# Two fused transformer blocks: the expert stage's small experts in four column tiles, its activations in other buffers, rows flipped and weight blocks refetched earlier

## The chip, the cores and the metric

The program runs on one core of a Trainium2 chip. The metric is the device time of one execution in microseconds (us); less is better. The times shown are three executions of the kernel before, and one more execution was taken with the hardware profiler.

## What is computed

Two transformer blocks on 512 rows of width 1024, in float32. The change touches only the mixture of experts of the second block, which is

```python
def moe(x, w_router, b_router, w_up, b_up, w_down, b_down):
    xf = x.reshape(-1, D)
    logits = (xf @ w_router + b_router).astype(jnp.float32)
    top_v, top_i = lax.top_k(logits, TOP_K)          # TOP_K = 4 of 32 experts
    w = jax.nn.softmax(top_v, axis=-1)
    ...
    h = lax.ragged_dot(xs, w_up, sizes) + b_up[sorted_e]     # w_up: 1024 x 2048 for each expert
    g, lin = jnp.split(h, 2, axis=-1)
    g = jnp.minimum(g, SWIGLU_LIMIT)
    lin = jnp.clip(lin, -SWIGLU_LIMIT, SWIGLU_LIMIT)
    act = g * jax.nn.sigmoid(SWIGLU_ALPHA * g) * (lin + 1.0)
    y = lax.ragged_dot(act, w_down, sizes) + b_down[sorted_e] # w_down: 1024 x 1024 for each expert
    y = y * w.reshape(-1)[order][:, None].astype(y.dtype)
    return jax.ops.segment_sum(y, tok, num_segments=n).reshape(B, T, D)
```

The 512 rows make 2048 row-expert pairs. Counted with the reference's fixed inputs, twelve experts have more than 64 rows (149, 143, 130, 127, 126, 121, 101, 101, 87, 87, 82 and 74), nine have at most 32, and the other eleven lie between 33 and 63. Nothing of this is known when the program is built: the counts are worked out on the chip, and the program branches on them.

## The kernel before, in words

**Weight blocks.** An expert's weights are read once, as 12 blocks of 1 MiB (128 x 2048 float32): eight of `w_up` and four of `w_down`. All 32 experts' blocks run through one ring of eight raw buffers, so that block n+8 can be fetched only when the buffer of block n is free; `refill(n)` issues that fetch, on SyncE's (SP's) queue, in the order of the program. The raw buffers are halves of four tiles: `b1` holds blocks 0 and 1 of the ring, `pp` 2 and 3, `b3` 4 and 5, `b0` 6 and 7 (the profile writes all but `pp` as `b`). I call an expert's blocks F0 to F11 for a small expert and E0 to E11 for a large one.

**Places.** `order` sorts the experts by row count and gives each a place 0 to 31. Place 0 is expert 0's, a large one here. Large experts (over 64 rows) take the even places 2, 4, ... by falling count, small ones the odd places by rising count. `places` then runs `nP` pairs (here 11) of a small step `few(1 + 2t, paired)` and a large step `expert(2 + 2t)`, in nested `If`s on `nP`, and after them the remaining small experts one after the other (`rest`, a binary tree of `If`s, here from pair 11 on, and a last one). By the counts above, pairs 0 to 8 have a small expert of at most 32 rows, and pairs 9 and 10 one of 33 and 36.

**The small step** multiplies in float32, the expert's 64 rows standing in TensorE as weights and the block moving through: two column tiles of 64 columns side by side, 256 columns of the block each (`halves`). Right after a block's matmuls its buffer is refilled. Its activations are transposed into `hf`, which lies in tile `y`, the tile from which `finish` scatters results with an adding indirect DMA.

**The large step** works in split precision: ScalarE rounds a block to `wh`, VectorE makes the rest `wl` (`split`, lines 219 and 220), into one of four pairs of buffers (`pairs`, by n % 4), and TensorE takes three products for each of four 128-row pieces (`part`). Blocks are split two ahead of their use; E0 and E1 are split in the small step before (`unfold` at i = 10, 11). A split frees the raw buffer: E2 to E11 are refilled behind their split, but E0 and E1 only in the large step, behind E2's and E3's. `ahead` transposes ("flips") the next step's gathered rows: a large expert's rows at i = 8 and 9 of the small step. In pairs 0 to 3 (`SECOND`) the large step also computes rows 128 to 159 of its expert with `second`, in float32 and four column tiles of 32, from the raw block, and so keeps each raw buffer until then.

**Order of the work.** The program is written with a framework that schedules each engine's instructions and puts in the waits. The lines that touch the change:

```python
            if i < 10:
                self.split(*self.pairs[(n + 2) % self.PAIRS], self.raw(n + 2))
                if not two:
                    self.refill(n + 2)
            if i < 2 and not two:
                self.refill(n)
```

Of the kernel before, what the change touches and what calls it, by code (L numbers as in the profile page):

```python
# [25 lines left out]
NE, TT = 32, 128  # L26
# [131 lines left out]
class K:  # L158
# [944 lines left out]
    RAW, PAIRS = 8, 4  # L1103
# [38 lines left out]
    def moe(self):  # L1142
        tc, nc, a = self.tc, self.nc, self.a
        with ExitStack() as es:
# [52 lines left out]
            for n in range(2):  # L1197
                self.unfold(n)
# [10 lines left out]
    def places(self, srt):  # L1209
# [41 lines left out]
        pairs(0)  # L1251
# [106 lines left out]
    def finish(self, e, big):  # L1358

        nc, m = self.nc, self.m  # L1360
        sl, i = m["sl"][e // 4 % 2], e % 4
        if big:
            for c in range(2):
                nc.scalar.activation(m["y"][0][:, 512 * c:512 * c + 512], self.bank(e, 8 + c), AF.Copy, scale=sl["w"][:, i:i + 1])
            self.scatter(m["y"][0], sl, i)
        else:
            for c in range(2):
                p, w = self.bank(e, 8 + c), sl["w"][:64, i:i + 1]
                nc.scalar.activation(m["y"][0][:64, 512 * c:512 * c + 256], p[:64, :256], AF.Copy, scale=w)
                nc.vector.tensor_scalar(m["y"][0][:64, 512 * c + 256:512 * c + 512], p[64:, :256], w, None, op0=OP.mult)  # L1370
            self.scatter(m["y"][0], sl, i, 64)
# [44 lines left out]
    def expert(self, e, two=False):  # L1416
# [7 lines left out]
        for i in range(12):  # L1424
            n = e * 12 + i
            if i < 10:
                self.split(*self.pairs[(n + 2) % self.PAIRS], self.raw(n + 2))
                if not two:
                    self.refill(n + 2)
            if i < 2 and not two:  # L1430
                self.refill(n)
# [5 lines left out]
            if i == 0 and e:  # L1437
                self.finish(e - 1, False)
# [6 lines left out]
        self.finish(e, True)  # L1445
# [16 lines left out]
    def second(self, i, e):  # L1462
# [6 lines left out]
        act, hf = [m["y"][0][:, 256 * a:256 * a + 256] for a in range(2)]  # L1469
# [35 lines left out]
    def halves(self, p, x, i, e):  # L1505
# [5 lines left out]
        o = p[:64, :256], p[64:, :256]  # L1511

        cut = lambda w, n: self.cut(w, up, j, n, 2)
        if up and kh == 0:
            b = self.bup.bitcast(F32)[:, 512 * (j // 2):512 * (j // 2) + 512]
            for n in range(2):
                nc.tensor.matmul(o[n], self.m["one"][e % 2].bitcast(F32)[:, j % 2, :64], cut(b, n), start=True, stop=False)
        w = self.raw(e * 12 + i).rearrange("p (k f) -> p k f", k=4)
        for k in range(4):
            for n in range(2):  # L1520
                nc.tensor.matmul(o[n], x(4 * kh + k), cut(w[:, k], n), start=not up and kh == k == 0, stop=kh == 1 and k == 3)  # L1521

    def few(self, e, paired=False, second=False):
# [3 lines left out]
        xf, act = m["xf"], m["act"][0][:, :512]  # L1527
        hf = m["y"][0][:, :512].rearrange("p (t a r) -> p t a r", t=4, a=2)
        h = lambda k: hf[:, k % 2, k // 2] if k < 4 else hf[:, k % 2 + 2, k // 2 - 2]
        for i in range(12):  # L1530
            n = e * 12 + i
            self.halves(self.bank(e, i), (lambda k: xf[:, k]) if i < 8 else h, i, e)
            self.refill(n)
            if i > 9 and (paired or e == NE - 1):
                self.unfold(n + 2)
            if i == 0 and e and e % 2 == 0:
                self.finish(e - 1, False)
            self.ahead(e, i, 8, paired)
            if i == 3 and second:
                self.further(e + 1)  # L1540
            if i in (3, 5, 7):
                j = i // 2
                pg, pl = [self.bank(e, k)[:, :256] for k in (0, 2)] if j == 1 else \
                    [self.bank(e, i)[:, 128 * k:128 * k + 128] for k in range(2)]
                self.gated(pg, pl, self.side(act, j, 64))
            if i in (5, 8, 9):
                t0, t1 = {5: (0, 2), 8: (2, 3), 9: (3, 4)}[i]
# [3 lines left out]
                nc.vector.tensor_copy(hf[:, t0:t1].rearrange("p t a r -> p t (a r)"), p[:, :t1 - t0])  # L1551
            if e == NE - 1 and i == 6:
                self.last_rows(e)
        if e % 2 == 0:
            self.finish(e, False)
# [3 lines left out]
    def ahead(self, e, i, at, both):  # L1559
# [5 lines left out]
        for f in [e + 2] * (i == 2) + [1] * (i == 1 and e == 0):  # L1565
            if f < NE:
                self.gather(m["xg"][f % 2], m["sl"][f // 4 % 2], f % 4, 64 if f % 2 or at == 8 and e else 128)
# [167 lines left out]
    def order(self, c):  # L1735
# [13 lines left out]
        gt = S2[:, 160:222].rearrange("p (a e) -> p a e", a=2)  # L1749
        col = [S2[:, 284 + i:285 + i] for i in range(12)]  # L1750
        kc, big, q1, g, sb, far, ex = col[:7]
        r4 = S2[:, 296:298]
        r, na = [r4[:, i:i + 1] for i in range(2)]
# [45 lines left out]
        v.memset(of[:, 3:7], 0.0)  # L1799
# [139 lines left out]
```

## Time and profile before

| what | us |
|---|---|
| three executions: median (lowest to highest) | 2599.25 (2596.93 to 2601.3) |
| the profiled execution's own time | 2600.15 |
| its span, first to last instruction | 2598.1 |
| pairs 0 to 3, from the first small step's first matmul (window in Rows 2) | 335.8 |
| pair 4 | 72.8 |
| pairs 5 to 9 | 348.2 |
| pair 10 and the wait behind it | 84.7 |
| the nine small experts behind the pairs | 285.1 |

The span is divided by the first matmul of a pair's small step (line 1517), which can be read off TensorE's timeline. Everything ahead of 1385.4 us is the first block, the attention of the second, routing and place 0.

### The profile page before, as it was taken

The page shows a single profiled execution, that of the slowest core. Times are in us where ns is not written, and L with a number is a line of the kernel's source. Part 1 is how long each engine was busy: PE and PEld are TensorE (multiplying, and loading weights), DVE is VectorE, ACT ScalarE, POOL GpSimd, SP SyncE. Part 2 cuts the span into 40 slices and gives each one's busy share as a digit, 9 for nine tenths or more (in the row PEclk, how much of TensorE's full clock was granted, in tenths as well). Part 3 has the DMA queues.
Part 4 walks back from the last instruction along what each step waited for, and adds up shares of the span by engine and source line. Part 5 has one row for each costly group of instructions (what it writes and reads, how often), then busy time and mean ns, then how long its engine had stood idle before and what let it go on. Part 6 is the DMA issues. An engine that isn't in the chain of part 4 may idle for free. (4 is left out here: it accounts for less than half of the span.)

```text
span 2598.1 us, 41846 instructions
## 1 busy us (share of the span) xinstructions
PE 2425.4 (93%) x17042; PEld 1941.2 (75%) x17042; DVE 1326.2 (51%) x2473; ACT 1043.5 (40%) x1578; POOL 174.5 (7%) x184
## 2 busy tenths in 40 slices
PE   7999999999999999999989999999999999788888
PEld 5789987898898898898976676666666666554557
DVE  6767753344333344557585466445656666121135
ACT  5755552223223324557353344334444444111133
POOL 0021100000000000000010010110001000000000
PEclk9999999999999999999979999999999999899999
DMA  4122222322222222220378889989999999799990
GB/s 160 65 90 78 74 70 89 127 86 88 98 93 86 98 70 83 75 71 17 109 271 324 305 317 333 341 301 367 381 378 392 385 403 373 294 399 400 407 376 33
DMA packets 86474, 552.63 MB, mean 213 GB/s; under 512 B 11799, under 2 KB 12951, under 8 KB 24936
## 3 DMA queue, kind: packets, MB, share of 16 engines
q1 hardware_dynamic: 71280, 508.33, 50.6%
q0 software_dynamic: 8352, 29.76, 4.7%
q10 hardware_dynamic: 6616, 11.53, 1.3%
q8 instruction: 142, 2.33, 0.4%
q14 instruction: 84, 0.69, 0.1%
HBM read 530.03 MB, written 19.55 MB: 212 GB/s over the span
## 5 line engine op out<-in xcount | busy, mean ns | idle before, releaser
L245 PE MATMUL mm<-b,wh 128*128 128x512 f32 (+1 forms) x1840 | 512.8, 365 | 1.7 <-ACT b L222 0.8
L245 PEld LDWEIGHTS mm<-b,wh 128*128 128x128 f32 x1840 | 328.8, 190 | 65.4 <-issue 3.4
L245 PE MATMUL mm<-b,wl 128*128 128x512 f32 (+2 forms) x920 | 335.2, 365 | 1.3 <-DVE wl L205 1.3
L245 PE MATMUL mm<-wh,b 128*128 128x256 f32 x1488 | 284.3, 287 | 1.5 <-DVE b L675 0.8
L205 DVE TENSOR_TENSOR wl<-raw,wh 128x2048 fp32r<-128x2048 f32 x81 | 185.5, 2290 | 176.2 <-ACT wh L204 176.2
L204 ACT ACTIVATE wh<-raw 128x2048 fp32r<-128x2048 f32 x81 | 155.1, 1915 | 261.2 <-PE mm L245 248.8
L245 PEld LDWEIGHTS mm<-wh,b 128*128 128x128 f32 x1488 | 235.9, 191 | 4.6 <-DVE b L675 1.2
L245 PE MATMUL mm<-wl,b 128*128 128x256 f32 x744 | 213.0, 286 | 1.0 <-DVE wl L205 1.0
L220 DVE TENSOR_TENSOR wl<-b,wh 128x2048 fp32r<-128x2048 f32 x74 | 169.2, 2288 | 65.4 <-ACT wh L219 62.4
L245 PEld LDWEIGHTS mm<-b,wl 128*128 128x128 f32 (+1 forms) x920 | 174.6, 190 | 31.8 <-DVE wl L205 2.2
L1521 PE MATMUL lg<-b,xf 128*64 128x256 f32 x1280 | 154.3, 389 | 14.7 <-DMA b<-w_up 10.1
L219 ACT ACTIVATE wh<-b 128x2048 fp32r<-128x2048 f32 x74 | 141.0, 1908 | 61.8 <-DMA b<-w_up 30.8
L245 PEld LDWEIGHTS mm<-wl,b 128*128 128x128 f32 x744 | 141.9, 191 | 2.5 <-DVE wl L205 1.3
L1521 PEld LDWEIGHTS lg<-b,xf 128*64 128x64 f32 x1280 | 94.3, 139 | 65.7 <-DMA b<-w_up 15.9
L1521 PE MATMUL lg<-b,b 128*64 128x256 f32 x1024 | 130.7, 394 | 7.5 <-DMA b<-w_dn 7.2
L213 POOL TENSOR_TENSOR rs<-rm,c_nhalf 128x1 f32<-128x1 f32 (+3 forms) x52 | 53.0, 1021 | 1158.9 <-DVE rm L211 1150.6
L1521 PEld LDWEIGHTS lg<-b,b 128*64 128x64 f32 x1024 | 76.0, 141 | 49.1 <-issue 11.5
L1345 ACT ACTIVATE sg<-mm,seven 128x128 f32<-128x128 f32 (+2 forms) x48 | 21.8, 455 | 223.2 <-PE mm L1521 180.9
L1521 PE MATMUL mm<-pp,xf 128*64 128x256 f32 x640 | 84.3, 388 | 4.6 <-DMA pp<-w_up 4.5
L1347 DVE SCALAR_TENSOR_TENSOR sg<-lg,sg 128x256 f32<-128x256 f32 (+1 forms) x48 | 19.2, 399 | 127.6 <-ACT sg L1346 127.6
L1521 PE MATMUL mm<-b,xf 128*64 128x256 f32 x640 | 74.8, 383 | 7.0 <-DMA b<-w_up 7.0
L1345 ACT ACTIVATE sg<-lg,seven 128x256 f32<-128x256 f32 (+1 forms) x48 | 21.7, 452 | 146.1 <-PE lg L1521 118.4
(534 smaller groups left out, 4597.9 us busy)
## 6 DMA issues: line engine op xcount, KB each, us to landing
b<-w_up SPq DMA_DIRECT2D x190, 1024.0 KB, 6.7
b<-w_dn SPq DMA_DIRECT2D x96, 1024.0 KB
pp<-w_up SPq DMA_DIRECT2D x64, 1024.0 KB, 13.4
raw<-w_in SPq DMA_DIRECT2D x39, 1024.0 KB, 4.9
pp<-w_dn SPq DMA_DIRECT2D x32, 1024.0 KB, 14.2
raw<-w_up SPq DMA_DIRECT2D x16, 1024.0 KB, 5.8
raw<-w_down SPq DMA_DIRECT2D x16, 1024.0 KB, 4.8
raw<-w_out SPq DMA_DIRECT2D x8, 1024.0 KB, 4.8
```

The lines of the kernel that those rows point to most:

```text
L204: nc.scalar.activation(wh, raw, AF.Copy)
L205: nc.vector.tensor_tensor(wl, raw, wh.bitcast(F32), op=OP.subtract)
L213: self.nc.gpsimd.tensor_tensor(r, m, self.c["nhalf"][:, :n], op=OP.pow)
L219: nc.scalar.activation(hi, src, AF.Copy)
L220: nc.vector.tensor_tensor(lo, src, hi.bitcast(F32), op=OP.subtract)
L245: self.nc.tensor.matmul(ps, l, r, start=(i == 0), stop=(i == n - 1))
L1345: nc.scalar.activation(sg, pg, AF.Relu, scale=-1.0, bias=m["seven"][:rows, 0:1])
L1347: nc.vector.scalar_tensor_tensor(sg, pg, 7.0, sg, op0=OP.min, op1=OP.mult)
L1521: nc.tensor.matmul(o[n], x(4 * kh + k), cut(w[:, k], n), start=not up and kh == k == 0, stop=kh == 1 and k == 3)
```

## The change

- `few` takes a number `of` of column tiles. With `of=4` it keeps 32 rows and sends 128 columns of the block to each of four tiles (`pieces`, in place of `halves`); `finish` then evacuates four pieces of 32 x 128 for each bank and scatters 32 rows.
- `order` also counts the experts of at most 32 rows, and `places` runs nested `If`s on `nT` (the smaller of that count and `nP`) with `of=4`; then it loads `nP` and goes through a binary tree of `If`s for the pairs that are left, with `of=2`, and then `rest` as before.
- In a small step that is paired, the large expert's rows are flipped at i = 4 and 5 instead of 8 and 9.
- E0 and E1 are refilled right behind their split in the small step, if `second` doesn't need them.
- `hf` lies in `act`, not in `y`; `second`'s activations lie in `actb`, not in `y`.

```diff
+    RAW, PAIRS, LEAD = 8, 4, 2
-    def unfold(self, n):
+    def unfold(self, n, keep=False):
         wh, wl = self.pairs[n % self.PAIRS]
         self.split(wh, wl, self.raw(n))
-        if n % 12 > 1 or n >= NE * 12:
+        if not keep:
             self.refill(n)
...
-        nP = load(1, 15)
-        def pairs(t):
+        nT = load(3, 15)
+        def pair(t, of):
+            self.few(1 + 2 * t, True, t < self.SECOND, of)
+            self.expert(2 + 2 * t, t < self.SECOND, of)
+        def tiny(t):
             if t < NE // 2 - 1:
-                with tc.If(nP > t):
-                    self.few(1 + 2 * t, True, t < self.SECOND)
-                    self.expert(2 + 2 * t, t < self.SECOND)
-                    pairs(t + 1)
+                with tc.If(nT > t):
+                    pair(t, 4)
+                    tiny(t + 1)
+        def pairs(lo, hi):
+            if hi - lo > 1:
+                mid = (lo + hi) // 2
+                with tc.If(nT < mid):
+                    pairs(lo, mid)
+                with tc.If(nP > mid):
+                    pairs(mid, hi)
+            else:
+                with tc.If(nT < lo + 1):
+                    with tc.If(nP > lo):
+                        pair(lo, 2)
...
-        pairs(0)
+        tiny(0)
+        nP = load(1, 15)
+        pairs(0, NE // 2 - 1)
         rest(0, NE // 2 - 1)
...
+        rows, y = 128 // of, m["y"][0]
+        w = sl["w"][:rows, i:i + 1]
+        for c in range(2):
+            for g in range(of):
+                p, o = self.bank(e, 8 + c)[rows * g:rows * g + rows, :512 // of], y[:rows, 512 * c + 512 // of * g:][:, :512 // of]
+                if g % 2:
+                    nc.vector.tensor_scalar(o, p, w, None, op0=OP.mult)
+                else:
+                    nc.scalar.activation(o, p, AF.Copy, scale=w)
+        self.scatter(y, sl, i, rows)
...
-            if i < 10:
-                self.split(*self.pairs[(n + 2) % self.PAIRS], self.raw(n + 2))
-                if not two:
-                    self.refill(n + 2)
-            if i < 2 and not two:
+            if i + self.LEAD < 12:
+                self.unfold(n + self.LEAD, keep=two)
+            if i < self.LEAD and not e:
                 self.refill(n)
...
-        act, hf = [m["y"][0][:, 256 * a:256 * a + 256] for a in range(2)]
+        act, hf = [m["actb"][0][:, 256 * a:256 * a + 256] for a in range(2)]
...
+        r = 128 // of
+        o = [p[r * g:r * g + r, :512 // of] for g in range(of)]
...
         for k in range(4):
-            for n in range(2):
-                nc.tensor.matmul(o[n], x(4 * kh + k), cut(w[:, k], n), start=not up and kh == k == 0, stop=kh == 1 and k == 3)
+            for g in range(of):
+                nc.tensor.matmul(o[g], x(4 * kh + k), self.cut(w[:, k], up, j, g, of), start=not up and kh == k == 0,
+                                 stop=kh == 1 and k == 3)
...
-        hf = m["y"][0][:, :512].rearrange("p (t a r) -> p t a r", t=4, a=2)
+        hf = m["act"][0][:, 512:512 + 256 * q].rearrange("p (t a r) -> p t a r", t=2 * q, a=of)
...
-            if i > 9 and (paired or e == NE - 1):
+            if paired and i + self.LEAD > 11:
+                self.unfold(n + self.LEAD, keep=second)
...
-            self.ahead(e, i, 8, paired)
+            self.ahead(e, i, 4 if paired else 8, paired)
...
+        v.tensor_scalar(gt[:, 2], key[:, 1:], 32 * 32 + 31.5, None, op0=OP.is_lt)
+        v.tensor_tensor(of[:, 3:4], nP, tiny, op=OP.min)
```

Three places of the order of instructions. The first is SP's queue, in pair 5: the last fetches of the small step's refills and those that follow in the large step. `b_12343` (now `b_12345`) holds the ring's blocks 6 and 7, `b_12206` blocks 0 and 1, `pp` blocks 2 and 3, so with `w_dn` they are E8 and E9 for `b_12206`, E10 and E11 for `pp`; the row that sets up each transfer is left out. Before:

```order
L1122 DMA b_12343<-w_up 128x2048
L1122 DMA b_12343<-w_up 128x2048
L1379 TENSOR_LOAD ovi
L1122 DMA pp<-w_dn 128x2048
L1122 DMA b_12206<-w_dn 128x2048
L1122 DMA pp<-w_dn 128x2048
L1122 DMA b_12206<-w_dn 128x2048
```

And in the changed program:

```order
L1122 DMA b_12345<-w_up 128x2048
L1122 DMA b_12206<-w_dn 128x2048
L1122 DMA b_12345<-w_up 128x2048
L1122 DMA b_12206<-w_dn 128x2048
L1396 TENSOR_LOAD ovi
L1122 DMA pp<-w_dn 128x2048
L1122 DMA pp<-w_dn 128x2048
```

The fetches were issued in the order E6, E7, E10, E8, E11, E9; now it is E6, E8, E7, E9, E10, E11, and E8's stands ahead of E7's.

The second place is ScalarE in pair 5, from the end of the small step on (`wh`, `raw` and `b_12224` are the four pairs' upper halves; `b_12232` the flipped rows of the large expert; L1369, now L1387, evacuates the small step's result in `finish`). Before:

```order
L219 ACTIVATE b_12232<-tr 128x512
L219 ACTIVATE wh<-b_12206 128x2048
L219 ACTIVATE b_12232<-tr 128x512
L219 ACTIVATE wh<-b_12206 128x2048
L1369 ACTIVATE b_12234<-lg,s0w 64x256 x2
L219 ACTIVATE raw<-pp 128x2048
L219 ACTIVATE b_12224<-pp 128x2048
```

Now:

```order
L219 ACTIVATE b_12232<-tr 128x512
L1362 ACTIVATE sg<-mm,seven 128x64
L1363 ACTIVATE sg<-sg,seven 128x64
L1387 ACTIVATE b_12234<-lg,s0w 32x128 x4
L219 ACTIVATE wh<-b_12206 128x2048 x2
L219 ACTIVATE raw<-pp 128x2048
L219 ACTIVATE b_12224<-pp 128x2048
```

Both flips have moved ahead of E0's split, and so have the evacuations of the small step, of which there are four now.

The third place is TensorE in the same small step (L1303, now L1320, are the flips of the 128 gathered rows `xg`; the gather of the next large expert's rows into `xg` waits for them). Before, behind the up-projection's four double blocks:

```order
L1521 MATMUL mm<-pp,xf 64x256 x16
L1521 MATMUL lg<-b_12225,b_12234 64x256 x8
L1303 MATMUL tr<-c_ident,xg 128x128 x4
L1550 MATMUL tr<-c_ident,b_12234 128x128
L1521 MATMUL lg<-b_12225,b_12234 64x256 x8
```

Now, in the third double block:

```order
L1535 MATMUL mm<-b_12206,xf 32x128 x16
L1320 MATMUL tr<-c_ident,xg 128x128 x4
L1535 MATMUL mm<-b_12206,xf 32x128 x16
L1568 MATMUL tr<-c_ident,b_12234 128x128
L1531 MATMUL mm<-bup,one_12238 32x128 x4
```

The flips stand five blocks earlier, and each block has twice as many matmuls, half as wide.

## Rows read from the trace of the kernel before

**Rows 1.** The page's second part: GB/s moved, in 40 slices of 65 us.

```profile
GB/s 160 65 90 78 74 70 89 127 86 88 98 93 86 98 70 83 75 71 17 109 271 324 305 317 333 341 301 367 381 378 392 385 403 373 294 399 400 407 376 33
```

**Rows 2.** Stretches: length, busy PE, PEld, DVE, ACT, POOL; PEclk, DMA share, GB/s.

```profile
1385.40:1721.20 335.80, 325.12 (x3290) 228.43 (x3290) 188.90 (x338) 144.01 (x172) 31.13 (x24) 0.97 0.87 321
1721.20:1794.00 72.80, 67.71 (x401) 46.87 (x401) 41.55 (x62) 32.03 (x33) 7.21 (x5) 0.95 0.97 370
1794.00:2142.20 348.20, 324.84 (x1953) 227.97 (x1952) 204.88 (x272) 162.71 (x165) 30.41 (x20) 0.98 0.99 384
2142.20:2226.90 84.70, 67.91 (x401) 46.85 (x401) 41.54 (x58) 32.93 (x34) 6.59 (x5) 0.91 0.90 337
2226.90:2512.00 285.10, 244.56 (x1996) 152.46 (x1996) 55.07 (x174) 32.32 (x74) 18.01 (x15) 0.97 0.99 392
```

**Rows 3.** TensorE's timeline in pair 5: start, length, what; in brackets the wait ahead.

```profile
1794.00 0.65 PE L1517 MATMUL lg<-bup,one 128*64 128x256 f32 x4
1794.48 3.62 PE L1521 MATMUL lg<-b,xf 128*64 128x256 f32 x32
...
1818.83 0.50 PE L1316 MATMUL mm<-bup,one 128*128 128x512 f32 x1
...
1821.43 0.56 PE L1322 MATMUL mm<-wl,b 128*128 128x512 f32 x1 [1.83 <-DVE wl L220]
...
1850.63 0.50 PE L1322 MATMUL mm<-wl,h 128*128 128x512 f32 x1 [2.35 <-DVE wl L220]
...
1856.16 0.50 PE L1322 MATMUL mm<-wl,h 128*128 128x512 f32 x1 [1.27 <-DVE wl L220]
```

**Rows 4.** TensorE in pair 0: two blocks of the four-tile float32 product in `second`.

```profile
1419.08 2.12 PE L1482 MATMUL pv<-b,xs 128*32 128x128 f32 x64
```

**Rows 5.** ScalarE's timeline: the split of E0 in pair 5 and in pair 1.

```profile
1817.14 1.91 ACT L219 ACTIVATE wh<-b 128x2048 fp32r<-128x2048 f32 x1 [3.91 <-DMA b<-w_up]
...
1491.84 1.91 ACT L219 ACTIVATE wh<-b 128x2048 fp32r<-128x2048 f32 x1 [4.86 <-DMA b<-w_up]
```

**Rows 6.** DMA in 1816.5:1824, with the gather of 128 rows (q0); a small step's first 5 us.

```profile
DMA packets 510, 3.15 MB, mean 419 GB/s; under 512 B 62, under 2 KB 62, under 8 KB 190
...
q0 software_dynamic: 144, 0.52, 17.4%
...
1795.00:1800.00 5.00, 5.00 (x50) 3.34 (x48) 0.42 (x1) 0.98 (x2) 2.54 (x2) 1.00 0.63 116
```

**Rows 7.** ScalarE in pair 5: the splits of E10 (into raw) and E8 (into wh).

```profile
1843.80 1.92 ACT L219 ACTIVATE raw<-pp 128x2048 fp32r<-128x2048 f32 x1 [1.78 <-PE lg L1322]
1845.62 1.90 ACT L219 ACTIVATE wh<-b 128x2048 fp32r<-128x2048 f32 x1
```

**Rows 8.** Behind pair 10: TensorE's timeline, line 1243's branches in 2216:2223, a window.

```profile
2211.84 2.96 PE L1322 MATMUL mm<-b,h 128*128 128x512 f32 x12
2226.92 1.12 PE L1517 MATMUL lg<-bup,one 128*64 128x256 f32 x4 [12.12 <-DVE one L1286]
2229.47 6.25 PE L1521 MATMUL lg<-b,xf 128*64 128x256 f32 x32 [1.43 <-SPq L1243]
...
L1243 PEldq COMPARE_BRANCH  x2: 4552/4556/4560, 2216.9 to 2221.7; - x2
...
2215.00:2235.00 20.00, 6.65 (x32) 3.86 (x34) 0.29 (x1) 0.52 (x1) 2.54 (x2) 0.57 0.33 67
```

**Rows 9.** Single lines (ns min/median/max): a 32 x 128 evacuation, a small operation of the routing.

```profile
L1502 ACT ACTIVATE b<-pv,s2w x16: 359/361/363, 1460.4 to 1719.3; 32x128 f32<-32x128 f32 x16
...
L1760 DVE TENSOR_SCALAR b<-b x1: 162/162/162, 1331.0 to 1331.0; 128x31 f32<-128x31 f32 x1
```

**Rows 10.** TensorE's timeline: the starts of pair 1, of its large step, of pair 2.

```profile
1467.41 0.65 PE L1517 MATMUL lg<-bup,one 128*64 128x256 f32 x4
...
1496.73 0.68 PE L1459 MATMUL tr<-c_ident,b 32*128 32x32 f32 x8 [4.08 <-DVE b L220]
...
1550.93 0.65 PE L1517 MATMUL lg<-bup,one 128*64 128x256 f32 x4
```

More of the change, by code (lines that the diff above doesn't have):

```diff
@@ L1196, in moe @@
                 self.fetch(n)
-            for n in range(2):
-                self.unfold(n)
+            for n in range(self.LEAD):
+                self.unfold(n, keep=True)
             self.select(0)
@@ L1356, in bank, with finish @@
         return mm[(s + i % 2) % 4]
-    def finish(self, e, big):
+    def finish(self, e, of=2):
         nc, m = self.nc, self.m
         sl, i = m["sl"][e // 4 % 2], e % 4
[L1362 to L1371, printed above, removed]
+        rows, y = 128 // of, m["y"][0]
[8 more added lines that the diff above has]
+        self.scatter(y, sl, i, rows)
     def numbers(self, e):
@@ L1414, in last, with expert @@
             self.split(self.y[0][:64, cc], self.y[1][:64, cc], y)
-    def expert(self, e, two=False):
+    def expert(self, e, two=False, of=2):
         nc, m = self.nc, self.m
@@ L1437, in expert @@
             if i == 0 and e:
[L1438 removed]
+                self.finish(e - 1, of)
             self.ahead(e, i, 6, False)
@@ L1444, in expert @@
             self.second_finish()
-        self.finish(e, True)
+        self.finish(e, 1)
     def cut(self, w, up, j, n, of):
@@ L1503, in second_finish, with pieces @@
         self.scatter(m["actb"][0], m["sl"][2], 0, 32)
-    def halves(self, p, x, i, e):
+    def pieces(self, p, x, i, e, of):
         nc = self.nc
@@ L1510, in halves @@
         kh, j = (c % 2, c // 2) if up else ((i - 8) // 2, 0)
-        o = p[:64, :256], p[64:, :256]
-        cut = lambda w, n: self.cut(w, up, j, n, 2)
+        r = 128 // of
+        o = [p[r * g:r * g + r, :512 // of] for g in range(of)]
         if up and kh == 0:
             b = self.bup.bitcast(F32)[:, 512 * (j // 2):512 * (j // 2) + 512]
-            for n in range(2):
-                nc.tensor.matmul(o[n], self.m["one"][e % 2].bitcast(F32)[:, j % 2, :64], cut(b, n), start=True, stop=False)
+            for g in range(of):
+                nc.tensor.matmul(o[g], self.m["one"][e % 2].bitcast(F32)[:, j % 2, :r], self.cut(b, up, j, g, of), start=True, stop=False)
@@ L1518, in halves @@
         w = self.raw(e * 12 + i).rearrange("p (k f) -> p k f", k=4)
         for k in range(4):
-            for n in range(2):
-                nc.tensor.matmul(o[n], x(4 * kh + k), cut(w[:, k], n), start=not up and kh == k == 0, stop=kh == 1 and k == 3)
-    def few(self, e, paired=False, second=False):
+            for g in range(of):
+                nc.tensor.matmul(o[g], x(4 * kh + k), self.cut(w[:, k], up, j, g, of), start=not up and kh == k == 0,
+                                 stop=kh == 1 and k == 3)
@@ L1525, in few @@
+    def few(self, e, paired=False, second=False, of=2):
         nc, m = self.nc, self.m
         self.numbers(e)
-        xf, act = m["xf"], m["act"][0][:, :512]
-        hf = m["y"][0][:, :512].rearrange("p (t a r) -> p t a r", t=4, a=2)
-        h = lambda k: hf[:, k % 2, k // 2] if k < 4 else hf[:, k % 2 + 2, k // 2 - 2]
+        rows, q = 128 // of, 4 // of
+        xf, act = m["xf"], m["act"][0][:, :1024 // of]
+        hf = m["act"][0][:, 512:512 + 256 * q].rearrange("p (t a r) -> p t a r", t=2 * q, a=of)
+        h = lambda k: hf[:, k % q + q * (k // 4), k % 4 // q]
@@ L1530, in few @@
         for i in range(12):
             n = e * 12 + i
-            self.halves(self.bank(e, i), (lambda k: xf[:, k]) if i < 8 else h, i, e)
+            self.pieces(self.bank(e, i), (lambda k: xf[:, k, :rows]) if i < 8 else h, i, e, of)
             self.refill(n)
-            if i > 9 and (paired or e == NE - 1):
+            if paired and i + self.LEAD > 11:
+                self.unfold(n + self.LEAD, keep=second)
+            if e == NE - 1 and i > 9:
                 self.unfold(n + 2)
             if i == 0 and e and e % 2 == 0:
-                self.finish(e - 1, False)
@@ L1554, in few @@
         if e % 2 == 0:
-            self.finish(e, False)
+            self.finish(e)
         if e == NE - 1:
@@ L1566, in ahead @@
             if f < NE:
-                self.gather(m["xg"][f % 2], m["sl"][f // 4 % 2], f % 4, 64 if f % 2 or at == 8 and e else 128)
+                self.gather(m["xg"][f % 2], m["sl"][f // 4 % 2], f % 4, 64 if f % 2 or at != 6 and e else 128)
         if i == 2 and e + 1 < NE:
@@ L1748, in order @@
         key, t32, P, P2 = [S2[:, o:o + n] for o, n in ((0, 32), (32, 32), (64, 32), (96, 64))]
-        gt = S2[:, 160:222].rearrange("p (a e) -> p a e", a=2)
+        gt = S2[:, 160:253].rearrange("p (a e) -> p a e", a=3)
         col = [S2[:, 284 + i:285 + i] for i in range(12)]
         kc, big, q1, g, sb, far, ex = col[:7]
-        r4 = S2[:, 296:298]
-        r, na = [r4[:, i:i + 1] for i in range(2)]
+        r4 = S2[:, 296:299]
+        r, na, tiny = [r4[:, i:i + 1] for i in range(3)]
         of = self.ovf
```

13 lines of the change are left out of this document (7 added, 6 removed).

## The prediction

> **What bounds the kernel now.** I read the slices of the page first: up to the twentieth the core moves some 90 GB/s and the change touches nothing; then the experts begin and the traffic stands between 300 and 407 GB/s until the end [rows 1]. A table of stretches cut at the pairs' first matmuls divides that half [rows 2]. The reader is to see two regimes. In pairs 0 to 3 TensorE is busy 325.1 of 335.8 us and the DMA engines 0.87 of the time: TensorE sets the pace, 83.95 us a pair. In pairs 5 to 9, 69.64 us each, the DMA share is 0.99 and TensorE has 4.7 us a pair to spare; the nine small experts behind the pairs are at 0.99 as well. There the weights' stream sets the pace or nearly so. Between pair 10 and those nine TensorE stands still for 12.12 and then 1.43 us [rows 8].
>
> Then TensorE's own timeline in one pair [rows 3]. The small step lasts from 1794.00 to 1818.83, all of it busy. What comes next decides everything: the large step's first block must have landed and been split. ScalarE stood idle for E0's landing and began its split at 1817.14, 23.1 us after the small step's start; in pair 1 at 1491.84, 24.4 us after it (small step from 1467.41) [rows 5, 10]. Over the six such rows of pairs 5 to 10 that distance is 22.7 to 23.1, mean 22.9; over the four of pairs 0 to 3 it is 22.8 to 24.4, mean 23.85. So the small step's 24.8 us of matmuls lie beside the landing of F8 to F11 and E0, which takes almost as long: a fetch can begin only when F0's buffer is free, and in the first 5 us the results' scatter and the next gather share the engines, which are at 0.63 and move 116 GB/s [rows 6].
>
> **The four tiles.** Two blocks take 3.62 us in two column tiles [rows 3] and took 2.12 in four, in `second` [rows 4]; so a block costs 1.06 instead of 1.81, and twelve 9.0 us less. Nine pairs have at most 32 rows, but the work removed lies ahead of E0's landing, not on the path. What remains of it is that F0 is free earlier: 0.43 + 1.06 against 0.48 + 1.81, 0.8 us.
>
> **E0's landing, otherwise.** Two things push it back. The flips moved to i = 4 and 5 release `xg`, and the 128-row gather of the next large expert goes out some 12 us earlier, ahead of E0 and no longer behind it: 0.52 MB at 17.4% of 7.5 us, 1.3 us of all engines [rows 6]. And on ScalarE the small step's evacuations now stand ahead of E0's split: four of 0.36 us [rows 9], which begin when F11, a block ahead of E0 on the queue, has landed and been multiplied. A block takes 2.5 us at 419 GB/s, and 1.06 + 1.44 is that, so I charge 0.3. Together +0.8 us (bounds -0.8, if the gather fits in beside, to +2.1, all of gather and evacuations).
>
> **Pairs 0 to 3.** In pair 1 TensorE began the large step with E0 wholly split at 1497.4 and reached the next pair at 1550.93, 53.5 us [rows 10], the wait of 4.08 ahead of it and the slower matmuls after that wait included. That wait was for a flip queued behind E0's split on ScalarE and VectorE, which the earlier flips remove; the split itself (4.2 us, from 1.91 and a VectorE pass of 2.3) remains. A pair becomes 23.85 + 0.8 + 4.2 + 53.5 = 82.4: 1.5 less, four times, **6 us** (bounds: 36, if E0 came as early as TensorE is done, and a loss of 5 by the late landing).
>
> **The order of refills, pairs 4 to 8.** In pair 5's large step TensorE waited 2.35 and 1.27 us for lower halves [rows 3], those of E8 and E9. The splits show why: ScalarE split E10 at 1843.80, after waiting for its pair of buffers, and E8 only at 1845.62 [rows 7], as E10 had been fetched first. With E0 and E1 refilled in the small step, E8 and E9 come in order and these 3.6 us go. The large step from E0's landing on is then 69.64 - 22.9 - 3.6 = 43.1, and the pair 43.1 + 22.9 + 0.8 = 66.8. The new order has a price: SP holds E7's fetch behind E8's, which waits for E0's split. Five blocks stand in the queue then, so nothing starves. The stream bounds the gain: 384 GB/s over 69.64 us is 26.7 MB, 63.8 us at 419 GB/s, but with the scatters' slow 5 us it will not reach that; I take 67.4, between that and today's 69.64. Pair 4 and four of 69.64 are 351.4 and become 337.0: **14.4 us** (bounds 3, if only pair 4 gains, and 32).
>
> **Pairs 9 and 10** keep two column tiles, whose matmuls no longer lie under E0's landing by much: 67.6 each, against 69.64 and 72.5 up to pair 10's last matmul, 2214.8: **6.9 us** (0 to 12).
>
> **The new branches.** Leaving the nested `If`s on nT at pair 9 and going through the tree costs three bodies to be skipped: the rest of the nest, pairs 0 to 6, pairs 7 and 8. Behind pair 10 there are three today (the rest of the nest, 0 to 6, 7 to 10) and there will be three again. [...] By the stream, the engines were at 0.33 for 20 us, 13.4 us idle, less the 1.9 that a common boundary loses [rows 6]: 11.5. A full ring and a scatter already done give some back in the next pair, so I take **13 us lost** (11.5 to 17). [...]
>
> **Small things.** Two more operations of 0.16 us and a wider sum in the routing chain: 0.4 lost [rows 9]. `hf` away from the scatter: VectorE waited for scatters in a few small steps, in the DMA-bound part behind the pairs or under E0's landing, so nothing; without that cover, the wait would be on the path of F8's matmuls.
>
> **The sum.** 6 + 14.4 + 6.9 - 13 - 0.4 = 13.9 us. The profiled execution took 2600.15, 2.05 more than its span and 0.9 above the median: **2586 us**.
>
> **The rivals.**
> 1. The new skips outweigh it. If the stream already bounds pairs 4 to 10 (share 0.99 [rows 2] speaks for that; the 2.35 and 1.27 us of waiting, and the half-idle first 5 us, against), they stay as they are, TensorE's pairs gain at most 3, and the 13 us stand: 2610. It decides where the pairs give back less than 8 us. Chance 0.18.
> 2. The parts cancel: pairs 4 to 10 give 10 us instead of 21, so 2597. Chance 0.17.
> 3. The four tiles pay where TensorE sets the pace: E0 lands up to 6 us earlier in pairs 0 to 3 than I think, since the fetches are issued faster, some 36 us in place of 6: 2556. Against it, the engines were at 1.0 for most of the wait [rows 6]. Chance 0.11; that they pay in all nine pairs, 81 us, in the forecast's 13 behind the skips, 2532, 0.01. [...]
> 4. The skips cost little, since the queue's eight blocks are consumed meanwhile: 2573. For it, the DMA went on for some 6 us of the gap; against it, the 13.4 us of idle engines [rows 8]. Chance 0.08.
> 5. My forecast, 2576 to 2594: 0.45.
>
> **How the numbers follow.** A measurement of this kernel tells about 0.2%, 5.2 us, from no change (its three executions spread over 4.4). Forecast, 3 and 4 are faster, less 0.03 for forecasts that fall just inside: faster 0.62. Rival 2 and those, 0.20. Rival 1: slower 0.18. The range of 8 in 10 leaves out most of rival 3 and the worst of rival 1: 2566 to 2608.
>
> **What the profile after would show.** In pairs 0 to 8 the small step's matmuls are done after some 17 to 20 us and TensorE then waits for E0, whose split starts 23 to 25 us after the step's start; if it starts at 18, rival 3 is right. The waits for E8's and E9's lower halves are gone, E8 is split ahead of E10, and pairs 5 to 8 are 66 to 68.5 us long at a DMA share of 1.0; if they are at 69 or more, rival 1 holds. Ahead of pair 9 there is a second stretch with a DMA share near 0.33 and a wait of TensorE of 12 to 15 us; if it is under 5, rival 4 is right. My prediction is wrong altogether if the landing is not what the large step waits for.

## The result, and the profile after

The changed kernel took 2570.57 us (median of 5 runs, 2566.17 to 2575.94) against 2599.25 before: ratio 0.99, 95% interval 0.9883 to 0.9916. It is 28.7 us faster, about twice the 13.9 forecast; 2570.57 lies inside the range, 4.6 above its lower end, and outside the forecast's own 2576 to 2594. Its profiled execution has a span of 2568.8 us.

The stretches of the changed kernel, cut as in [rows 2] at the first matmul of a pair's small step (now line 1531): pairs 0 to 3, pair 4, pairs 5 to 8, the new stop ahead of pair 9, pairs 9 and 10, the stop behind them, the small experts.

```profile
1380.40:1699.28 318.88, 290.98 (x4114) 216.77 (x4113) 183.60 (x344) 143.64 (x180) 28.26 (x24) 0.95 0.90 337
1699.28:1766.10 66.82, 57.41 (x607) 43.37 (x606) 41.03 (x61) 32.71 (x35) 5.19 (x5) 0.95 1.01 392
1766.10:2035.28 269.18, 232.88 (x2393) 176.52 (x2392) 161.01 (x223) 130.48 (x140) 19.57 (x16) 0.90 1.01 397
2035.28:2048.84 13.56, 0.00 (x1) 0.03 (x1) 0.29 (x1) 0.69 (x1) 1.59 (x1) 0.62 0.51 129
2048.84:2182.20 133.36, 129.57 (x784) 90.53 (x784) 81.71 (x109) 63.90 (x65) 14.19 (x7) 0.99 0.97 386
2182.20:2195.98 13.78, 0.00 (x0) 0.03 (x1) 0.16 (x1) 0.69 (x1) 1.60 (x1) 0.62 0.58 167
2195.98:2481.00 285.02, 242.44 (x1982) 152.80 (x1982) 55.40 (x175) 32.18 (x73) 17.98 (x15) 0.96 0.99 389
```

The two traces differ by 2598.1 - 2568.8 = 29.3 us. By stretch: 5.0 ahead of pair 0 (1380.40 against 1385.37), 16.9 in pairs 0 to 3, 16.7 in pairs 4 to 8 (336.0 against 352.7), 7.6 in pairs 9 and 10 (133.4 against 140.9), less 13.6 for the new stop, 1.7 for the longer stop behind pair 10 and 1.6 behind it.

In pairs 4 to 8 the profile shows what was forecast of the refills. TensorE in pair 5 (the answer to [rows 3]): it now waits inside the small step, for the blocks themselves, and no longer for E8's and E9's lower halves. One sign did not come: I expected the small step's matmuls done after 17 to 20 us and a wait for E0 behind them, and F11's last matmuls end at 1789.2, 23.1 us after the pair's start.

```profile
1766.35 1.93 PE L1535 MATMUL lg<-b,xf 128*32 128x128 f32 x64
...
1783.65 1.93 PE L1535 MATMUL lg<-b,b 128*32 128x128 f32 x32 [2.81 <-DMA b<-w_dn]
...
1792.27 0.50 PE L1339 MATMUL mm<-wh,b 128*128 128x512 f32 x1 [0.92 <-ACT wh L219]
1794.60 0.80 PE L1339 MATMUL mm<-wl,b 128*128 128x512 f32 x1 [1.82 <-DVE wl L220]
```

ScalarE in the same pair (the answer to [rows 5] and [rows 7]): E0 and E1 are split at 1790.33, 24.2 us after the pair's start at 1766.10; E8 (into wh) at 1812.21, well ahead of E10 (into raw) at 1819.19.

```profile
1790.33 3.79 ACT L219 ACTIVATE wh<-b 128x2048 fp32r<-128x2048 f32 x2
...
1812.21 1.91 ACT L219 ACTIVATE wh<-b 128x2048 fp32r<-128x2048 f32 x1
...
1819.19 1.90 ACT L219 ACTIVATE raw<-pp 128x2048 fp32r<-128x2048 f32 x1
```

Pairs 0 to 3 are where the forecast was short. Means in us, read off TensorE's and ScalarE's timelines of each kernel (experiments included, below); the two middle columns of figures divide a pair of 0 to 3 at the start of E0's split:

| kernel | pairs 0 to 3, each | start to E0's split | from there to the next pair | pairs 4 to 8, each |
|---|---|---|---|---|
| before | 83.95 | 23.86 | 60.09 | 70.54 |
| changed | 79.72 | 26.03 | 53.69 | 67.20 |
| changed, once more | 78.95 | 25.26 | 53.69 | 67.30 |
| two tiles | 83.14 | 24.75 | 58.39 | 68.19 |
| two tiles, late flips | 83.81 | 23.70 | 60.11 | 68.59 |
| four tiles, late flips | 79.42 | 25.74 | 53.69 | 67.04 |
| four tiles in pairs 0 to 3 only | 79.62 | 25.93 | 53.69 | 67.63 |
| refills late | 78.86 | 25.18 | 53.68 | 70.87 |
| buffers back | 79.45 | 25.76 | 53.69 | 69.75 |
| order of refills alone | 83.23 | 24.14 | 59.08 | 68.05 |

The reader is to see that E0 did not come earlier in the changed kernel: its split starts 2.2 us later than before (1.4 in the second profile). All of the gain lies behind it, 6.4 us a pair.

### The profile page after: what moved, and what is told of

Read it like the earlier page. It is cut to its first block, busy times and chain, and to the rows that moved or that the text cites. A ratio compares the mean times of both kernels' runs of the same rounds, so it can differ in the third digit from the quotient of the medians.

```text
span 2568.8 us, 45746 instructions
## 1 busy us (share of the span) xinstructions
PE 2347.1 (91%) x18896; PEld 1917.2 (75%) x18896; DVE 1317.4 (51%) x2484; ACT 1043.5 (41%) x1596; POOL 169.3 (7%) x184
## 5 line engine op out<-in xcount | busy, mean ns | idle before, releaser
L1535 PE MATMUL lg<-b,xf 128*32 128x128 f32 (+1 forms) x1856 | 125.1, 321 | 17.2 <-DMA b<-w_up 11.3
L1535 PE MATMUL lg<-b,b 128*32 128x128 f32 (+1 forms) x1600 | 110.9, 339 | 31.9 <-DMA b<-w_dn 24.8
L1535 PEld LDWEIGHTS lg<-b,xf 128*32 128x32 f32 (+1 forms) x1856 | 85.9, 122 | 47.9 <-DMA b<-w_up 16.4
L1535 PEld LDWEIGHTS lg<-b,b 128*32 128x32 f32 (+1 forms) x1600 | 72.9, 129 | 55.5 <-issue 26.4
L1362 ACT ACTIVATE sg<-mm,seven 128x64 f32<-128x64 f32 (+3 forms) x48 | 20.9, 436 | 153.1 <-PE mm L1535 129.4
L1339 PE MATMUL mm<-wh,b 128*128 128x512 f32 x192 | 73.7, 454 | 7.4 <-ACT wh L219 7.4
L1535 PE MATMUL mm<-pp,xf 128*32 128x128 f32 (+1 forms) x928 | 67.3, 317 | 8.0 <-DMA pp<-w_up 5.0
L245 PE MATMUL mm<-wh,mg 128*128 128x256 f32 x384 | 71.2, 283 | 0.8 <-DVE b L675 0.4
```

Source lines behind the costliest of these rows:

```text
L245: self.nc.tensor.matmul(ps, l, r, start=(i == 0), stop=(i == n - 1))
L1339: nc.tensor.matmul(p, s[:, kk], w[:, k], start=not up and kk == j == 0, stop=kk == KC - 1 and j == len(terms) - 1)
L1362: nc.scalar.activation(sg, pg, AF.Relu, scale=-1.0, bias=m["seven"][:rows, 0:1])
L1535: nc.tensor.matmul(o[g], x(4 * kh + k), self.cut(w[:, k], up, j, g, of), start=not up and kh == k == 0, stop=kh == 1 and k == 3)
```

## The experiments

**First theories.** A (order): the gain behind E0's split in pairs 0 to 3 comes from what no longer stands behind that split on ScalarE and VectorE, the flips above all; the four tiles bring next to nothing, the order of refills brings pairs 4 to 10 their gain, the skips cost 13 us. B (stream, my rival 3): the four tiles free raw buffers sooner. C: the flips' place in the step.

**Two tiles.**

```diff
-                    pair(t, 4)
+                    pair(t, 2)
```

> The changed kernel with two column tiles of 64 rows in every pair; flips, refills, buffers and branches stay changed. Theory A (order): what pairs 0 to 3 gained (79.7 us a pair, 83.95 before) lies behind E0's split, 53.7 us from it to the next pair in place of 60.1, because the flips no longer stand behind that split; E0 itself did not come earlier (26.0 us after the pair's start, 23.85 before). Then two tiles cost only the 0.8 us of a later landing in each of nine pairs: pairs 0 to 3 near 80, pairs 5 to 8 near 68, about 2577 in all (2572 to 2581). Theory B (stream): the four tiles free the raw buffers sooner and so bring the blocks sooner; then pairs 0 to 3 go back to 83 and pairs 5 to 8 to 69, about 2594.

Measured: 2595.28 us, ratio to before 0.9975 (0.9963 to 0.9987). Theory A falls: nearly the whole gain went with the tiles. But B's reason falls too, for E0's split starts 24.75 us after the pair's start, no later than with four tiles. What is longer is the part behind it, 58.39 in place of 53.69. TensorE's timeline shows why. With two tiles, pair 1 (E0's split at 1494.54):

```profile
1490.57 3.70 PE L1535 MATMUL lg<-b,b 128*64 128x256 f32 x32
1494.20 0.68 PE L1474 MATMUL tr<-c_ident,b 32*128 32x32 f32 x8
...
1496.51 0.49 PE L1339 MATMUL mm<-wh,b 128*128 128x512 f32 x1 [1.20 <-ACT wh L219]
1498.83 0.79 PE L1339 MATMUL mm<-wl,b 128*128 128x512 f32 x1 [1.83 <-DVE wl L220]
...
1504.16 1.92 PE L1497 MATMUL pv<-b,xs 128*32 128x128 f32 x64
```

With four, pair 1 of the changed kernel (E0's split at 1484.67):

```profile
1479.49 1.06 PE L1474 MATMUL tr<-c_ident,b 32*128 32x32 f32 x8 [5.20 <-DMA b<-xs,s2i]
...
1485.82 1.08 PE L1497 MATMUL pv<-b,xs 128*32 128x128 f32 x32
1486.83 0.51 PE L1339 MATMUL mm<-wh,b 128*128 128x512 f32 x1
1487.27 1.06 PE L1497 MATMUL pv<-b,xs 128*32 128x128 f32 x26
1488.94 0.50 PE L1339 MATMUL mm<-wl,b 128*128 128x512 f32 x1 [0.61 <-DVE wl L220]
```

From E0's split to the first product with its lower half it is 4.29 us with two tiles and 4.27 with four. Meanwhile, with two, TensorE comes out of the small step just then and has nothing ready: VectorE copies the extra rows into place only behind both lower halves (line 1475, at 1501.18), and their products stand behind E0's. With four it had finished, and does the extra rows' products with E0 and most of those with E1 (line 1497, 58 of 64 matmuls) and the last biases beside the split. Windows of the two kernels, from E0's split on, two tiles first:

```profile
1494.54:1498.83 4.29, 1.26 (x8) 0.60 (x7) 2.29 (x1) 3.71 (x2) 0.00 (x0) 0.81 1.01 418
1498.83:1503.82 4.99, 4.99 (x11) 3.47 (x11) 4.81 (x5) 4.45 (x5) 0.00 (x0) 0.50 1.02 422
1503.82:1552.74 48.92, 48.92 (x571) 36.98 (x570) 32.62 (x49) 23.50 (x29) 3.79 (x2) 1.00 0.81 308
```

```profile
1479.49:1484.67 5.18, 5.18 (x59) 3.88 (x59) 1.62 (x5) 0.99 (x3) 0.00 (x0) 0.50 1.03 423
1484.67:1488.94 4.27, 3.61 (x62) 2.08 (x60) 2.69 (x3) 4.27 (x4) 1.39 (x1) 0.89 1.01 420
...
1488.94:1538.35 49.41, 49.41 (x503) 36.40 (x504) 35.36 (x49) 26.20 (x30) 1.00 (x1) 1.00 0.85 325
```

In the split's 4.3 us TensorE is busy 3.61 us with four tiles and 1.26 with two: 2.35 more is done. And the stretch at a granted clock of 0.50, which follows a wait of TensorE in either kernel (5.20 us with four tiles, 1.20 and 1.83 with two), lies ahead of E0's split with four tiles and behind it with two, on the path. What is left of 58.2 - 53.7 = 4.5 us, 2.2, is that clock: TensorE is busy that much longer behind the split, where the eleven products from E0's first lower half on take 4.99 us at 0.50 with two tiles and 2.84 at 1.00 (1488.94 to 1491.78) with four.

The clock is not the cause in every pair, though. Pair 3 of the two-tile kernel is like pair 1, but in pairs 0 and 2 the granted clock is 1.00 behind E0's split, and the part is as long (58.50 us in both, 58.20 and 58.37 in pairs 1 and 3). There three quarters of F11's own matmuls are done behind the split. Pair 0, from E0's split at 1410.13 on:

```profile
1410.13:1419.43 9.30, 8.92 (x73) 5.34 (x70) 6.45 (x7) 6.84 (x6) 0.00 (x0) 1.00 1.02 419
```

```profile
1414.86 2.81 PE L1535 MATMUL lg<-b,b 128*64 128x256 f32 x24
```

This is theory D: the four tiles pay where the large step has work that needs the raw block alone, as TensorE is then done with the small step before the split; with two tiles it is left with F11's matmuls or with a wait and half the clock.

**Flips at 8 and 9 again**, with four and with two tiles. With four, both flips still stand ahead of E0's split on ScalarE in the program's order; with two, the second stands between E0's and E1's splits.

```diff
-            self.ahead(e, i, 4 if paired else 8, paired)
+            self.ahead(e, i, 8, paired)
```

> The changed kernel with the large expert's flips at i = 8 and 9 again; four tiles stay. In the program's order both flips still stand ahead of E0's split on ScalarE, since with four tiles TensorE reaches them early. Theory A: what counts is that they stand ahead of it, so nothing changes: 2570 (2567 to 2574), E0's split to the next pair still 53.7 us in pairs 0 to 3. Theory C (the place of the flips in the step as such): pairs 0 to 3 lose their gain, 4 to 5 us each, about 2588.

> The changed kernel with two column tiles in every pair and the flips at i = 8 and 9: the second flip stands between E0's and E1's splits again, as before the change. Theory A: this pair of edits together carries pairs 0 to 3; they go back to some 84 us, and pairs 4 to 8 lose 1 us each: about 2570 + 4 x 4.2 + 5 + 4 = 2596. Theory B: it is no slower than the kernel with two tiles alone, about 2594 both. If flips and tiles are independent, it loses the sum of what each loses alone.

Measured: 2573.38 (0.9879, 0.9859 to 0.99) with four tiles, and 2599.03 (0.9995, 0.9984 to 1.0007) with two. So the flips' place is worth nothing beside four tiles and some 4 to 5 us beside two (0.9975 against 0.9995, intervals that just overlap): C falls, and of what A says of pairs 0 to 3 only this is left.

**One nest.** Left out of the diff: the load of `nP` in place of `nT`, and the call of the tree for the pairs that are left, which goes.

```diff
-                with tc.If(nT > t):
-                    pair(t, 4)
+                with tc.If(nP > t):
+                    pair(t, 4 if t < 9 else 2)
...
```

> The changed kernel with one nest of branches on nP, four tiles in pairs 0 to 8 and two in the later ones: which pairs these are is written into the program from this input's counts, so the choice is no longer worked out on the chip. The second way through skipped bodies is gone, its 13.6 us ahead of pair 9 with it. Theory A (the skips cost what the trace shows): 2570.6 - 13.6 = 2557 (2554 to 2560). Rival: the ring fills during the stop and gives back in pairs 9 and 10 (65.5 and 67.9 us where pairs 5 to 8 average 67.3), so at most 11 are won: 2560 to 2563. Rival: the stream does not stop for the branches, 2570.

Measured: 2562.61 us, 0.9855 (0.9837 to 0.9872) against 0.99 and 0.9905 for the change: 12 to 13 us by the ratios, 8 to 12 by the medians. TensorE's timeline of this kernel shows pair 9 begin right behind pair 8, and pair 8 with what follows it takes 68.01 us in place of 81.12:

```profile
2028.84 2.48 PE L1337 MATMUL mm<-b,h 128*128 128x512 f32 x10
2031.25 0.65 PE L1529 MATMUL lg<-bup,one 128*64 128x256 f32 x4
```

By its time alone this is the first rival's 2560 to 2563, above my 2554 to 2560. But pairs 9 and 10 take 134.0 us here and 133.4 in the changed kernel, so the stop gives nothing back: the reasons of both rivals fall.

**The changed kernel once more, refills late, buffers back, the order of refills with the buffers.** The second undoes the early refill of E0 and E1; the third puts `hf` and the extra rows' activations into `y` again; the fourth is two tiles, late flips and one nest.

```diff
-            if i < self.LEAD and not e:
+            if i < self.LEAD and not two:
...
-                self.unfold(n + self.LEAD, keep=second)
+                self.unfold(n + self.LEAD, keep=True)
```

```diff
-        act, hf = [m["actb"][0][:, 256 * a:256 * a + 256] for a in range(2)]
+        act, hf = [m["y"][0][:, 256 * a:256 * a + 256] for a in range(2)]
...
-        hf = m["act"][0][:, 512:512 + 256 * q].rearrange("p (t a r) -> p t a r", t=2 * q, a=of)
+        hf = m["y"][0][:, :256 * q].rearrange("p (t a r) -> p t a r", t=2 * q, a=of)
```

> The changed kernel once more, unchanged, as a yardstick for the kernels beside it: 2570.6 (2566 to 2576). The first matmul of pair 0 has stood anywhere from 1376 to 1388 us in six profiles of kernels that don't differ ahead of it, so the 5 us that the first comparison showed there are chance and will not come again; the pairs' lengths will, within 1 us.

> The changed kernel with E0 and E1 refilled in the large step again, behind E2's and E3's split, so that E10 is fetched ahead of E8. Theory A: four tiles pay in pairs 0 to 3, where this order doesn't apply, and the order of refills pays in pairs 4 to 10, where it saves the waits for E8's and E9's lower halves: pairs 5 to 8 go from 67.3 to about 70 us, pairs 9 and 10 from 65.5 and 67.9 to 69, in all 2570.6 + 5 x 2.7 + 5 = 2589 (2584 to 2594). Rival: with four tiles TensorE has 7 to 10 us of waiting a pair, the order costs nothing and the stream sets the pace alone: 2572.

> The changed kernel with hf and the activations of the extra rows in tile y again, from which the scatters read. Theory A: VectorE's copy into hf waits for the large step's scatter, which lands some 14 us into the small step; F10 and F11 land then, and TensorE waits for those and for the gathered extra rows anyway, so little is lost: 2573 (2570 to 2577). Rival: with four tiles the cover is gone; the copy waits 6 us, F8 to F11 are multiplied, and their buffers refilled, that much later, and E0's split with them: 3 us in each of eleven pairs, about 2600.

> Two column tiles in every pair, flips at i = 8 and 9, one nest of branches on nP as in the kernel before: of the change only the order of refills and the two buffers are left. Theory A: it gains what the order of refills gains in pairs 4 to 10, 14.4 + 6.9 less what the tiles bring there, about 2600 - 16 = 2584 (2580 to 2590); the kernel with two tiles and late flips that keeps the second way through skipped bodies was as slow as before the change, since the skips took that back. Rival: the order gains nothing by itself, 2599, and the skips cost nothing net.

Measured: 2574.21 (0.9905, 0.9878 to 0.9931) for the change; 2592.42 (0.9973, 0.9953 to 0.9993) with late refills; 2586.95 (0.9948, 0.9930 to 0.9966) with the buffers back; 2583.36 (0.9948, 0.9930 to 0.9966) for the last.

Late refills cost 18 us, in pairs 4 to 10 alone: 70.87 a pair from 4 to 8, pairs 0 to 3 as fast as ever. TensorE's timeline in pair 5 of that kernel has the two waits of [rows 3] for E8's and E9's lower halves again, beside four tiles:

```profile
1826.43 0.50 PE L1339 MATMUL mm<-wl,h 128*128 128x512 f32 x1 [2.22 <-DVE wl L220]
...
1831.95 0.50 PE L1339 MATMUL mm<-wl,h 128*128 128x512 f32 x1 [1.29 <-DVE wl L220]
```

The buffers missed my figure: 12.7 us lost by the medians, where I had expected 2573, 2 to 3 us lost. Pairs 4, 6 and 8 take 69.5 to 72.1 us (pair 8 without the stop), with E0's split at 26.2 to 28.5, pairs 5 and 7 keep 67.5 and 67.8. VectorE in pair 4 of the kernel with the buffers back, its copy into `hf`, and TensorE:

```profile
1723.33 0.29 DVE L1570 COPY b<-tr 128x128 f32<-128x128 f32 x1 [8.39 <-DMA acc<-b,s0i]
```

```profile
1715.94 1.25 PE L1535 MATMUL mm<-pp,xf 128*32 128x128 f32 x34
1724.53 0.36 PE L1860 MATMUL tr<-rwt,oh 128*128 128x6 bf16 x8 [7.34 <-DVE b L220]
```

The copy waits 8.39 us for the scatter; behind it in VectorE's queue stand a flip's split and the one-hot rows of the next slots (line 1858), which only the small steps of even pairs work out. TensorE's wait of 7.34 us ahead of line 1860 ends with that flip's split (its first one-hot rows had been loaded before), later matmuls of that line wait for the next one-hot rows, and F7 and all that follows stand behind them. E0 is not late: in pair 4 it landed 21.5 us after the pair's start, 23.5 in the changed kernel. But its split starts only at 28.5, behind the evacuations of the delayed small step.

**The order of refills alone; tiles in pairs 0 to 3 alone; the extra rows behind F11.** The first is the fourth kernel above with the buffers back, too.

```diff
-                    pair(t, 4)
+                    pair(t, 4 if t < self.SECOND else 2)
```

```diff
-            self.second_rows()
+            with self.tc.issue_after(self.mm.ins): self.second_rows()
```

In the second diff `self.mm` is the last matmul of the small step; the line that keeps it is left out. What the expectations call theory A was by then mended by D.

> Two column tiles, late flips, one nest on nP, and hf and the extra rows' activations in y as before: of the change only the order of refills is left. Theory A: with two tiles the scatter that VectorE's copy waits for is covered by TensorE's slower blocks, so the buffers bring little here and the order of refills gains by itself what it gained with the buffers, 15 us: 2585 (2580 to 2589). Rival: the buffers, worth 12.7 us with four tiles, bring as much with two; then the order alone is near 2596.

> The changed kernel with four column tiles in pairs 0 to 3 alone and two in pairs 4 to 8. Theory A: the four tiles pay where TensorE sets the pace and its small step's end, not E0's landing, released the large step; pairs 4 to 8 lose about 0.9 us each (67.2 to 68.1): 2572 + 4.5 = 2577 (2573 to 2581). Rival: four tiles free buffers sooner wherever the stream sets the pace; pairs 4 to 8 lose most of the 21 to 25 us that two tiles cost in all pairs, about 2588.

> The changed kernel with the transposes of the extra rows held, on TensorE, behind the small step's last block in pairs 0 to 3, so that F11's matmuls and the evacuations ahead of E0's split no longer wait for the gather of those rows (5.2, 3.4, 2.3 and 0.5 us). If those waits delay E0's split, it starts some 1 to 2 us earlier in pairs 1 and 2: 2572 - 3 = 2569 (2566 to 2572). Rival: E0 lands no earlier, or the gather still ends last ahead of the extra rows' first product: no change, 2572.

> The fastest version by the rows: the changed kernel with one nest of branches (four tiles in pairs 0 to 8, by this input's counts) and the transposes of the extra rows behind F11. If both gains hold and add, 2572 - 10 - 3 = 2559 (2553 to 2564); if the transposes bring nothing, 2562, as the one nest alone.

Measured: 2582.36 (0.9923, 0.9904 to 0.9942) for the order alone; 2570.61 (0.9889, 0.9872 to 0.9905) for four tiles in pairs 0 to 3 alone; 2573.85 (0.9890, 0.9871 to 0.9910) for the extra rows behind F11; 2556.33 (0.9834, 0.9816 to 0.9852) for that with one nest.

Four tiles in pairs 0 to 3 alone bring all that four tiles bring, as theory D has it; my range, 2573 to 2581, was missed, since the 0.9 us a pair that I charged in pairs 4 to 8 does not show in the medians. The place is shown by this; the reason is read from the traces. In pairs 0 to 3 TensorE also sets the pace, and no kernel here has one without the other; nor was one tried with two tiles and the extra rows' copy and products ordered ahead of E0's. Windows of that kernel, pairs 0 to 3 and 4 to 8, and then of two tiles everywhere:

```profile
1376.81:1695.29 318.48, 291.20 (x4113) 216.93 (x4113) 183.28 (x341) 143.45 (x180) 28.12 (x24) 0.95 0.90 337
1695.29:2033.44 338.15, 323.19 (x1969) 224.84 (x1968) 205.39 (x279) 161.45 (x165) 36.44 (x21) 0.99 1.01 394
```

```profile
1387.23:1719.80 332.57, 324.51 (x3289) 227.15 (x3289) 188.81 (x339) 143.80 (x172) 34.77 (x24) 0.98 0.87 324
1719.80:2060.77 340.97, 326.11 (x1969) 227.20 (x1968) 205.45 (x279) 161.21 (x165) 38.69 (x21) 0.98 1.01 391
```

In pairs 4 to 8, at a DMA share of 1.01, two tiles take 338.15 and 340.97 us and four take 336.0 and 336.5; by the medians four tiles there bring nothing. The extra rows behind F11 changed nothing that can be measured: E0's split came at 25.04 us, 1.0 and 0.2 earlier than in the two profiles of the change, and what follows took 0.5 longer (54.15). The rows say why: the stretch at half clock now lies behind the split in pairs 1 to 3. From E0's split in pair 1:

```profile
1489.61:1493.91 4.30, 4.30 (x47) 2.39 (x50) 2.72 (x3) 3.81 (x3) 1.39 (x1) 0.50 1.02 427
```

From the split to the next pair it is 53.69, 54.88, 54.22 and 53.81 us in pairs 0 to 3. The last kernel is the fastest, as far as its one nest makes it; its interval overlaps that of one nest alone.

The kernels form a ladder from before to the change, one edit to a step; each ratio is to the kernel before on the same chip:

| edit added | ratio (95%) | step, us (difference x 2600) |
|---|---|---|
| order of refills | 0.9923 (0.9904 to 0.9942) | -20 |
| other buffers | 0.9948 (0.9930 to 0.9966) | +6, intervals overlap |
| second way through skipped bodies | 0.9995 (0.9984 to 1.0007) | +12 |
| early flips | 0.9975 (0.9963 to 0.9987) | -5, intervals just overlap |
| four tiles in pairs 0 to 3 | 0.9889 (0.9872 to 0.9905) | -22 |
| four tiles in pairs 4 to 8 (the change) | 0.99, 0.9905 | +3 to 4, intervals overlap |

## Why the prediction was right, and where it was short

**Pairs 4 to 8** (forecast 14.4): 16.7 in the trace. The step was right in its mechanism and nearly in its size: the waits for E8's and E9's lower halves are gone, pairs 5 to 8 take 67.3 us where 67.4 was taken, and E0's split starts 23.9 us after their start where 22.9 + 0.8 = 23.7 was. Refilling late brings the waits and 18 us back.

**Pairs 9 and 10** (6.9): 7.6. **The new branches** (-13): -13.6 in the trace, 12 with the ladder. The stream's idle time gives 11.5 of it [rows 8, 6]; the 1.5 on top and the bound of 17 were my estimate, and no run shows them. The runs showed a stop of 13.56 us in which TensorE does nothing, and 8 to 13 us won without it. Rival 4, that the queue covers the skips, is wrong, as the kernel with one nest shows; that the measured time lies nearest to its 2573 is chance.

**Pairs 0 to 3** (6): 16.9 in one trace of the change, 20.0 in the other; the ladder has 22 for the tiles alone. This term was mis-sized, and the step that failed is the sum 23.85 + 0.8 + 4.2 + 53.5. It let TensorE stand for E0's split whatever the small step did, and counted the four tiles as hidden under E0's landing but for 0.8 us. Measured, it is 26.0 + 53.7: the 4.27 us from E0's split to its first lower half lie within the 53.7, for TensorE fills most of them with the extra rows, and the stretch at half clock, where there was one behind the split (in pair 1 before, 0.52 granted over 1497.33:1500.82), now lies ahead of it (0.50 over 1479.49:1484.67). (A block in four tiles took 0.97 us, 1.93 for two in pair 5, and not 1.06.) The hint was in the rows that I read: TensorE was busy 325.1 of 335.8 us [rows 2], and the small step's end and E0's split lay within 1 us of each other [rows 5, 10], so that neither hid the other. Rival 3 named the right place and the wrong reason.

**E0's landing** (+0.8): the split starts 2.2 us later in pairs 0 to 3 of the first trace and 1.4 in the second. The landing itself is only 0.4 and 0.7 later: E0 landed 24.2 and 24.5 us after the pair's start, where before the change ScalarE stood idle for it and began at 23.86. The rest, 1.8 and 0.7, is a wait that I priced at 0.3: the small step's evacuations ahead of the split on ScalarE. In pair 1 of the changed kernel, E0 had landed at 1482.15 (18.2 us from issue to landing), and the split follows the last evacuation without a wait of its own:

```profile
1484.40 0.36 ACT L1387 ACTIVATE b<-lg,s0w 32x128 f32<-32x128 f32 x1 [0.41 <-DVE b L1385]
1484.67 3.69 ACT L219 ACTIVATE wh<-b 128x2048 fp32r<-128x2048 f32 x2
```

It is so in pairs 1 to 3, 5 and 7 of this trace, by 0.5 to 4.0 us; in pairs 0, 4, 6 and 8 the landing comes last. So what I called the test of the whole, that the large step waits for E0's landing, holds in about half of the pairs. On TensorE the transposes of the extra rows, which wait for their gather (5.20 us in pair 1), stand ahead of F11's matmuls and so of these evacuations. With them behind F11, 0.4 us of such waiting is left, and nothing is gained, as the stretch at half clock then falls behind the split.

**`hf` away from the scatter** (nothing): right by itself, and only by itself. With two tiles the buffers bring nothing; with four they are worth some 11 to 13 us, since the four tiles take the cover away. The sentence on what happens without the cover was right, and I did not see that the same change removes it.

**Ahead of pair 0** (-0.4): 5.0 gained in the first trace. It is chance: over the 14 profiles of before, the change and the experiments pair 0 begins anywhere from 1376.0 to 1390.0 us, and it began at 1387.2 with two tiles, where nothing differs ahead of it.

## What to carry to other kernels

Where an engine's own work and the landing that it waits for end within a microsecond, neither is cover for the other; ask what the engine could do during the rest of the chain (here the split) if it were done earlier, what the order of its queue lets it do, and at which clock it comes out of a wait (here 0.50 behind one of 5.20 us). Edits are not to be priced one by one where one removes what hides the other: the buffers were worth nothing until the tiles were faster. And a choice between two shapes of a loop's body costs what the way around the other one's code takes: with the choice inside the nest that is there already, made from this input's counts, the kernel was 8 to 13 us faster.

## What the runs showed of the hardware

The same line's branch took from 34 ns to 5.2 us. In the stop ahead of pair 9 (rows of line 1246's instructions in 2034:2050, ns min/median/max, first and last start):

```profile
L1246 DVEq COMPARE_BRANCH  x4: 43/50/63, 2035.1 to 2044.6; - x4
L1246 PEldq COMPARE_BRANCH  x4: 68/2264/5196, 2037.8 to 2048.4; - x4
L1246 ACTq COMPARE_BRANCH  x4: 34/45/50, 2040.4 to 2048.4; - x4
```

On TensorE's queue the line took 68 ns at least and 5196 at most; the nest's own branch (line 1239) took 6025 there. No run here shows what the long ones wait for; the DMA part of the profile bears on it. In the stop's 14 us (2035:2049) two queues of the kind "instruction" moved 21 packets, and 3 in the 20 us ahead of it:

```profile
q14 instruction: 16, 0.13, 4.2%
q8 instruction: 5, 0.08, 2.9%
```

In each of TensorE's three long branches (6.0, 5.2 and 4.5 us) a 16 KB packet of q8 lands, the last one 1.3 to 1.5 us before the branch ends.

With two tiles, the pairs that the stream bounds came out uneven: in the kernel with the order of refills alone pairs 5 and 7 took 65.0 and 66.4 us and pair 6 71.6, in the one with the buffers too 65.1, 65.2 and 71.5, and with early flips (four tiles in pairs 0 to 3 alone) 65.9, 65.7 and 70.6. In the two profiles of the change pairs 5 to 8 lie between 66.0 and 68.4. The even pairs also work out the next slots; what makes the uneven lengths was not followed up, and stays open.
